# The first modulation's sums in chunks of two, modulation halves at other places, and attention units between the value blocks

## The chip, the cores and the metric

The kernel is one launch on one core of a Trainium2 chip. The metric is the device time of that launch in microseconds (us). TensorE is called PE below, VectorE DVE, ScalarE ACT, GpSimd POOL; SyncE (SP) issues nearly all of the transfers.

## The reference, cut to what matters

Two layers run over 384 tokens (128 of context, 256 latent) of 1024 channels. Each layer is a feed-forward block, a mixer with three head groups, and a second feed-forward block; nine modulation vectors per layer (from `c` for the latent tokens, from `c_ctx` for the context) scale and shift what goes in and gate what comes out.

```python
def _layer(x, cvec, lp, mixer):
    mod = jax.nn.silu(cvec) @ lp["ada_w"] + lp["ada_b"]
    sh1, sc1, g1, sh2, sc2, g2, sh3, sc3, g3 = jnp.split(mod[:, None, :], N_ADA, axis=-1)
    h = _rmsnorm(x, lp["norm_g"][0]) * (1.0 + sc1) + sh1
    x = x + 0.5 * g1 * _swiglu(h, lp["ffn_w1"][0], lp["ffn_w3"][0], lp["ffn_w2"][0])
    h = _rmsnorm(x, lp["norm_g"][1]) * (1.0 + sc2) + sh2
    y, ctx = mixer(h)
    x = x + g2 * y
    h = _rmsnorm(x, lp["norm_g"][2]) * (1.0 + sc3) + sh3
    x = x + 0.5 * g3 * _swiglu(h, lp["ffn_w1"][1], lp["ffn_w3"][1], lp["ffn_w2"][1])
    return x, ctx
```

The mixer projects `h` to a gated long convolution (Hyena, by Fourier transforms), a neighbourhood attention (kind "N", 6 heads, with a learned bias and a mask) and a windowed grouped-query attention (kind "G", 6 query heads), and projects their outputs back.

## The kernel before, in words

**Matmuls.** Every large fp32 matmul is three products of split operands (`mm3`, lines 305 to 307): high by high, low by high, high by low. A weight tile arrives in a `raw` buffer, ACT copies it to `whi` (L142), DVE subtracts to make `wlo` (L143). There are four `raw` buffers and the split runs three tiles ahead of its use; a `raw` buffer comes free when `wlo` is made. Activations are split the same way into `mh` and `ml`. Results stand in 8 PSUM buffers of two tags, "a" and "b", handed out in rotation: a buffer's next user waits until all readers of the last one are done. Each engine runs its instructions in the order in which the code writes them.

**Start of layer 0.** `start(j, mid)` runs at the head (and, with `mid`, in the middle) of step j of the first feed-forward block's first eight steps, in which six output blocks are summed over eight pieces of 128 channels. It has to make the normalised, modulated input `mh[j]` of each step. The first two modulation vectors are made on PE, in chunks of columns (`CHUNK`, 3, 3 and 2 blocks of 128 columns), and for each chunk twice, q = 0 for the scale and q = 1 for the shift: `chunk_load` issues the weights, `chunk_rows` (L278) multiplies them into rows, ACT copies the rows (L280), `chunk_cols` (L289) turns them into columns, and DVE makes `gsc` (L299, L300) or `mod` (L296). The squares of x are summed by ACT (L326) and DVE (L328); `stats1` sums them over partitions on PE (`pss`, L341) and makes the reciprocal roots on DVE (L313 to L320), `stats2` spreads these over the partitions (`dg` L347, `pr` L353, `R` L355). `start_x` (L1131) multiplies x by `R`, and `start_h` (L1122) applies `gsc` and `mod` on ACT and splits the result.

**The other modulation vectors.** They are made on DVE, a "half" at a time (L206, one row of 1024 products summed for one of the two vectors). `ada_tick(rate)` adds 2·rate halves of credit and issues the whole ones at that place; `need` issues what is still missing when a piece of the next stage asks for it. `RATE` holds the rates of the feed-forward blocks, `MIXRATE` those in the mixer, `SLOTADA` those in attention slots 6 and later.

**The mixer.** It projects block by block (`project`, each with a callback after each weight tile); background generators (`add`, `work`, `drain`) fill in filter, rotary and normalisation work. The last projection is that of the neighbourhood values, `vN`. After it come the attention units, 12 of them (three pairs of heads, two query halves, N first, then G), one started per `slot()`. Slot s issues the mask transfers of unit s+2, the scores of unit s on PE with DVE's row minima (L896), the normalisation of unit s-1 on DVE (`un_norm`, L870 and L873), the transposes of unit s-2 on PE with ACT's copies (L934, L939), the value products of a finished pair (L957, L960), and then the exponentials of unit s on ACT (L913 for the context part, L919). Units of the first query half (n = 2) have a context part, those of the second (n = 1) have none. The output projection follows in three groups of blocks (`wout_block`); `update` (L385) adds each block into x, and `after` does the squares, `need` and the input of the next block.

Of the kernel before, what the change touches and what calls it, by code (L numbers as in the profile page):

```python
# [27 lines left out]
NSPL = 4  # L28
AHEAD = 3
NADAB = 3  # L30
RATE = ((0.76, 0.635), (0.63, 0.515), (0.69, 0.66), (0.065, 0))
MIXRATE = ((0.75, 0, 0, 0), (0.45, 0, 0, 0))
BUD = (1.55, 3.3, 1.3)
SLOTADA = (6, 0.3, 0.0)
CHUNK = ((0, 3), (3, 6), (6, 8))
TAGS = (True, False, True)
GA = 2
DLATE = 8
# [21 lines left out]
for _name, _w in (  # L60
    ("ada_b", DEPTH * NADA * KD), ("norm_g", DEPTH * 3 * KD), ("conv_w", DEPTH * 3 * 6), ("conv_b", DEPTH * 6),
    ("skip", DEPTH * 2), ("naq", DEPTH), ("nak", DEPTH), ("fb1", DEPTH), ("fb2", DEPTH), ("freq", DEPTH * 2),
    ("fscale", 3), ("sel", 2),
):
    SM[_name] = (_n, _w)
    _n += _w
# [13 lines left out]
def _build(ctx, tc, nc, A):  # L80
# [181 lines left out]
    def chunk_load(c):  # L262
        a, b = CHUNK[c]
        n = (b - a) * P
        for q in range(2):
            firsts[c, q] = [tt("adw", w=NT) for _ in range(KD)]
            for k, t in enumerate(firsts[c, q]):
                load(A["ada0"][q, k, :, a * P:b * P], t[:, :n])

    adm = {}  # L270

    def chunk_rows(c, q):
        a, b = CHUNK[c]
        n = (b - a) * P
        pm = ps("adm", "ab"[q])
        for k, t in enumerate(firsts.pop((c, q))):
            o = 32 * (k % 4)
            T.matmul(pm[o:o + 32, :n], ct[:, k], t[:, :n], start=(k < 4), stop=(k >= 4))  # L278
        rows = tt("adr", w=NT)
        S.activation(rows[:, :n], pm[:, :n], AF.Copy)  # L280
        adm[c, q] = pm, rows

    def chunk_cols(c, q):
        a, b = CHUNK[c]
        n = b - a
        pm, rows = adm.pop((c, q))
        o = pm[:, NT:NT + 2 * n]
        for i in range(n):
            T.matmul(o[:, 2 * i:2 * i + 2], rows[:, i * P:(i + 1) * P], small("sel", 0, 2), start=True, stop=True)  # L289
        o = o.rearrange("p (j v) -> p j v", v=2)  # L290
# [4 lines left out]
        if q:
            V.tensor_tensor(mod[0][:, 0, a:b], o, wide(small("ada_b", a, n)), op=ALU.add)  # L296
        else:
            t = gsc[0][:, 0, a:b]
            V.tensor_tensor(t, o, wide(small("norm_g", a, n)), op=ALU.mult)  # L299
            V.tensor_tensor(t, t, wide(gb0[:, a:b]), op=ALU.add)  # L300
        done.update((0, 1 - q, j) for j in range(a, b))
# [234 lines left out]
    def mixer(l, after):  # L536
# [328 lines left out]
        def un_norm(u):  # L865
            nm, n = u.nm, u.n
            sums, rec = nm[:, 4:4 + 2 * n], nm[:, 12:12 + 2 * n]
            if u.kind == "G":
                V.tensor_tensor(sums, sums, nm[:, 8:8 + 2 * n], op=ALU.add)
            V.reciprocal(rec, sums)  # L870
            for e in range(2):
                for c, (pr, w) in enumerate(u.pr[e]):
                    V.tensor_scalar(pr[:, :w], pr[:, :w], rec[:, e * n + c:e * n + c + 1], None, op0=ALU.mult)  # L873

        def un_score(u):
            i, n = u.i, u.n
# [191 lines left out]
        drain(q_it)  # L1068
        drain(k_it)
        drain(conv_it)  # L1070
        drain(filt_it)
        fft_it = add(fft())
# [59 lines left out]

    def start(j, mid=False):
        if mid:
            if j in (2, 5):
                c = (j + 1) // 3
                chunk_cols(c, 1)
                for k in range(*CHUNK[c]):
                    start_h(k)
        elif j == 0:  # L1140
            chunk_load(0)
            issue(3)
# [11 lines left out]
            for c in range(3):  # L1154
                start_x(c, R)
                start_h(c)
            ahead(2)
            issue(4)
            chunk_load(2)
            for c in range(3, KD):  # L1160
                start_x(c, R)
        elif j in (1, 4):
            chunk_rows((j + 2) // 3, 0)
        elif j in (2, 5):
            chunk_cols((j + 1) // 3, 0)
            chunk_rows((j + 1) // 3, 1)
        elif j == 6:
# [95 lines left out]
def _layout(I):  # L1263
# [32 lines left out]
    put("sel", (np.arange(P)[:, None] % 32 == np.arange(2)[None]).astype(f32))  # L1296
    a["sml"] = sml
    rows = np.concatenate(
        [
# [75 lines left out]
```

## Time and profile before

| | us |
|---|---|
| median of 3 runs | 1543.95 (1543.29 to 1543.99) |
| profiled execution | 1544.34 |
| its span in the trace | 1542.6 |
| PE busy | 1505.7 (98%) |
| DVE busy | 1139.4 (74%) |
| ACT busy | 672.6 (44%) |
| POOL busy | 70.7 (5%) |

The span is what the trace covers; the profiled execution's own time is 1.74 us more. Terms below are set against 1544.34, which is 0.39 us above the median of the three runs. In a row of the timeline the first number is the start in us from the start of the span, the second the duration; "L305" is a line of the kernel, `xN` the number of instructions in the row, and the bracket at the end is how long the engine was idle before it and which instruction released it. PEclk is TensorE's granted clock as a share of full speed: 1.00 is 2.4 GHz, 0.50 is 1.2 GHz.

### The profile page before, as it was taken

What the parts mean: (1) busy time and instruction counts of PE and PEld (TensorE: products, weight loads), DVE (VectorE), ACT (ScalarE), POOL (GpSimd) and SP (SyncE); (2) the same over time, 40 slices, a digit from 0 to 9 for tenths busy, and PEclk for the clock granted to TensorE, in tenths of its full rate; (3) what the DMA queues carried; (4) which work ended last, traced back from release to release, by engine and by line L of the source; (5) the groups of instructions that cost most, each with busy time, mean ns of one, the idle gap of its engine ahead of it and who ended that gap; (6) DMA issues with size and microseconds to landing.
All of it is one profiled execution on the core that took longest, in us unless ns stands there. A gap on an engine that the chain in (4) does not pass through costs nothing. (4 is left out here: it accounts for less than half of the span.)

```text
span 1542.6 us, 23084 instructions
## 1 busy us (share of the span) xinstructions
PE 1505.7 (98%) x8652; PEld 1444.0 (94%) x8652; DVE 1139.4 (74%) x2158; ACT 672.6 (44%) x1234; POOL 70.7 (5%) x181
## 2 busy tenths in 40 slices
PE   6999999999989999999999999999999999999999
PEld 3999999999768999999999999999996699999998
DVE  4489888879787788877758898787897767544344
ACT  4533333446566454333434433343556655433221
POOL 0000000013300000000000000000141000000000
PEclk9999999999999999999999999999999999999999
DMA  9656665664403446555544565566543034343442
GB/s 307 236 184 237 219 223 201 218 195 149 129 30 117 153 148 220 207 212 187 187 162 139 188 244 209 207 221 202 172 124 109 26 111 138 134 149 108 149 152 72
DMA packets 89733, 261.27 MB, mean 169 GB/s; under 512 B 10097, under 2 KB 27796, under 8 KB 89492
## 3 DMA queue, kind: packets, MB, share of 16 engines
q1 hardware_dynamic: 89236, 258.74, 49.1%
q8 instruction: 68, 1.11, 0.3%
q0 software_dynamic: 384, 1.05, 0.2%
q14 instruction: 45, 0.37, 0.1%
HBM read 257.13 MB, written 2.62 MB: 168 GB/s over the span
## 5 line engine op out<-in xcount | busy, mean ns | idle before, releaser
L143 DVE TENSOR_TENSOR wlo<-raw,whi 128x1024 fp32r<-128x1024 f32 (+2 forms) x352 | 394.4, 1126 | 122.6 <-ACT whi L142 122.5
L305 PE MATMUL up<-mh,whi 128*128 128x384 f32 (+1 forms) x1408 | 479.3, 340 | 4.9 <-ACT mh L142 4.9
L306 PE MATMUL up<-ml,whi 128*128 128x384 f32 (+1 forms) x1408 | 477.4, 339 | 0.7 <-DVE ml L143 0.4
L307 PE MATMUL up<-mh,wlo 128*128 128x384 f32 (+1 forms) x1408 | 477.3, 339 | 0.8 <-DVE wlo L143 0.6
L142 ACT ACTIVATE whi<-raw 128x1024 fp32r<-128x1024 f32 (+2 forms) x352 | 338.4, 974 | 264.4 <-PE dn L306 128.2
L206 DVE CUSTOM_DVE_ANT_0 junk<-adaw,cb,sml 128x1024 bf16<-128x1024 f32 x256 | 332.7, 1300 | 1.9
L305 PEld LDWEIGHTS up<-mh,whi 128*128 128x128 f32 x1408 | 265.8, 189 | 8.7 <-ACT mh L142 6.3
L306 PEld LDWEIGHTS up<-ml,whi 128*128 128x128 f32 x1408 | 265.6, 189 | 2.5 <-DVE ml L143 2.1
L307 PEld LDWEIGHTS up<-mh,wlo 128*128 128x128 f32 x1408 | 266.0, 189 | 2.1 <-DVE wlo L143 2.1
L305 PE MATMUL dn<-gh,whi 128*128 128x384 f32 x704 | 237.4, 337 | 0.0
L306 PE MATMUL dn<-gl,whi 128*128 128x384 f32 x704 | 237.2, 337 | 0.0
L307 PE MATMUL dn<-gh,wlo 128*128 128x384 f32 x704 | 237.1, 337 | 0.0
L142 ACT ACTIVATE gh<-t 128x384 fp32r<-128x384 f32 x76 | 39.9, 525 | 273.0 <-DVE t L485 263.3
L307 PEld LDWEIGHTS dn<-gh,wlo 128*128 128x128 f32 x704 | 132.2, 188 | 0.0
L305 PEld LDWEIGHTS dn<-gh,whi 128*128 128x128 f32 x704 | 132.2, 188 | 0.0
L306 PEld LDWEIGHTS dn<-gl,whi 128*128 128x128 f32 x704 | 132.2, 188 | 0.0
L305 PE MATMUL pj<-whi,mh 128*128 128x384 f32 (+1 forms) x240 | 80.1, 334 | 1.0 <-DVE hyt L362 1.0
L485 DVE TENSOR_TENSOR t<-up,t 128x384 f32<-128x384 f32 x72 | 40.0, 556 | 55.0 <-PE up L307 54.8
L307 PE MATMUL pj<-whi,ml 128*128 128x384 f32 (+1 forms) x240 | 78.3, 326 | 0.0
L306 PE MATMUL pj<-wlo,mh 128*128 128x384 f32 (+1 forms) x240 | 78.2, 326 | 0.0
L143 DVE TENSOR_TENSOR gl<-t,gh 128x384 fp32r<-128x384 f32 x76 | 42.5, 559 | 45.0 <-ACT gh L142 45.0
L326 ACT ACTIVATE sq<-xT 128x384 f32<-128x384 f32 x42 | 22.0, 525 | 100.6 <-DVE xT L385 99.3
(222 smaller groups left out, 1582.9 us busy)
## 6 DMA issues: line engine op xcount, KB each, us to landing
raw<-w SPq DMA_DIRECT2D x184, 512.0 KB, 4.4
adaw<-ada SPq DMA_DIRECT2D x128, 512.0 KB, 3.5
raw<-w SPq DMA_DIRECT2D x64, 448.0 KB, 4.3
raw<-win SPq DMA_DIRECT2D x48, 384.0 KB, 4.0
raw<-w13a SPq DMA_DIRECT2D x32, 384.0 KB, 4.0
adw<-ada SPq DMA_DIRECT2D x32, 192.0 KB, 4.3
raw<-woa SPq DMA_DIRECT2D x16, 384.0 KB, 3.2
nab<-nab SPq DMA_DIRECT2D x24, 192.0 KB, 2.5
```

The costliest lines, as they stand in the source:

```text
L142: S.activation(hi, src, AF.Copy)
L143: V.tensor_tensor(lo, src, hi.bitcast(F32), op=ALU.subtract)
L206: V.tensor_tensor_reduce(out=junk, in0=w, in1=cb[:, v, :], scale=scale, scalar=small("ada_b", (l * NADA + p) * KD + j), op0=ALU.mult, op1= ...
L305: T.matmul(out, ah, bh, start=start, stop=False)
L306: T.matmul(out, ah, bl, start=False, stop=False)
L307: T.matmul(out, al, bh, start=False, stop=stop)
L326: S.activation(sq, xT[j], AF.Square)
L485: V.tensor_tensor(t1, PQ[1][:, :NT], t1, op=ALU.mult)
```

## The change

Three places change. Line numbers of the changed kernel are 2 lower than before in the helpers (303 to 305 are the three products, 278 and 289 stay).

**The start.** There are four chunks of two column blocks. Both vectors of a chunk go through one PSUM buffer, so that one `chunk_rows` (16 matmuls of 256 columns) and one `chunk_cols` (2 matmuls) make both. The sum of squares and the statistics on DVE stand ahead of the first chunk's rows. In the loop the rows of chunk 1, 2, 3 stand in the middle of steps 1, 3, 5 and the columns, with `start_h`, at the head of steps 2, 4, 6.

```diff
-CHUNK = ((0, 3), (3, 6), (6, 8))
+CHUNK = ((0, 2), (2, 4), (4, 6), (6, 8))
...
+            r = stats1(V)
+            chunk_rows(0)
+            R = stats2(r)
             ada_tables(0)
-            chunk_rows(0, 0)
-            r = stats1(V)
-            chunk_cols(0, 0)
-            chunk_rows(0, 1)
-            R = stats2(r)
-            chunk_cols(0, 1)
+            start_x(0, R)
+            chunk_cols(0)
             ahead(1)
...
+        if j in (2, 4, 6):
+            chunk_cols(j // 2)
+            start_h(j)
+            start_h(j + 1)
```

PE's order from the start of the program to the first product of step 0, before (`adm` is the modulation's PSUM buffer, `adw` the weights, `adr` the rows, `up` an output block of the feed-forward block):

```order
L278 MATMUL adm<-adw,cb 32x384 x8
L341 MATMUL pss<-ones,accq 128x1 x3
L289 MATMUL adm<-sml,adr 128x2 x3
L278 MATMUL adm<-adw,cb 32x384 x8
L353 MATMUL pr<-dg,ones 128x384
L289 MATMUL adm<-sml,adr 128x2 x3
L305 MATMUL up_369<-mh_112,whi 128x384
```

and now:

```order
L339 MATMUL pss<-ones,accq 128x1 x3
L278 MATMUL adm<-adw,cb 32x256 x16
L351 MATMUL pr<-dg,ones 128x384
L289 MATMUL adm<-sml,adr 128x4 x2
L303 MATMUL up_358<-mh_112,whi 128x384
```

The sum of squares moved from between the two sets of rows to the head, and one set of columns is left between `pr` and the first product.

PE's order around the columns of the second chunk before: they stand in the middle of step 2, between products of the same `mh_114`.

```order
L306 MATMUL up_371<-ml_122,whi 128x384
L307 MATMUL up_371<-mh_114,wlo 128x384
L289 MATMUL adm<-sml,adr 128x2 x3
L305 MATMUL up_372<-mh_114,whi 128x384
L306 MATMUL up_372<-ml_122,whi 128x384
```

Now they stand directly ahead of the first product that uses `mh_114`, which is made from them:

```order
L304 MATMUL up_363<-ml_121,whi 128x384
L305 MATMUL up_363<-mh_113,wlo 128x384
L289 MATMUL adm<-sml,adr 128x4 x2
L303 MATMUL up_358<-mh_114,whi 128x384
L304 MATMUL up_358<-ml_122,whi 128x384
```

**The modulation halves of layer 0.** The rates of its first feed-forward block go up, the ticks in the slots go, and the blocks of the output projection's second and third group get a rate of 0.3.

```diff
-RATE = ((0.76, 0.635), (0.63, 0.515), (0.69, 0.66), (0.065, 0))
-MIXRATE = ((0.75, 0, 0, 0), (0.45, 0, 0, 0))
+RATE = ((0.82, 0.72), (0.63, 0.515), (0.69, 0.66), (0.065, 0))
+MIXRATE = ((0.75, 0, 0, 0.3), (0.45, 0, 0, 0))
-SLOTADA = (6, 0.3, 0.0)
...
-            if s >= SLOTADA[0]:
-                ada_tick(SLOTADA[1 + l])
```

DVE's order in layer 0's output projection before, ahead of the fourth block of x (`xT_87`; `wlo` are the low parts of the next weight tiles, `accq` the sum of squares):

```order
L143 TENSOR_TENSOR wlo<-raw,whi 128x768
L143 TENSOR_TENSOR wlo<-raw,whi 128x1024 x2
L143 TENSOR_TENSOR wlo<-raw,whi 128x768
L385 SCALAR_TENSOR_TENSOR xT_87<-po_4940,mod_106,xT_87 128x128
L385 SCALAR_TENSOR_TENSOR xT_87<-po_4940,mod_106,xT_87 128x256
L328 TENSOR_TENSOR accq<-accq,sq 128x384
```

and now (a half is the two rows of L205, with `junk` and `mod` as its outputs):

```order
L142 TENSOR_TENSOR wlo<-raw,whi 128x768
L205 ISA junk,mod_106<-adaw,cb,sml 128x1024
L205 ISA mod_106 128x1
L142 TENSOR_TENSOR wlo<-raw,whi 128x1024
L205 ISA junk,mod_106<-adaw,cb,sml 128x1024
L205 ISA mod_106 128x1
L142 TENSOR_TENSOR wlo<-raw,whi 128x1024
L142 TENSOR_TENSOR wlo<-raw,whi 128x768
L205 ISA junk,mod_106<-adaw,cb,sml 128x1024
L205 ISA mod_106 128x1
L383 SCALAR_TENSOR_TENSOR xT_87<-po_4982,mod_106,xT_87 128x128
```

Three halves now stand between these low parts and the fourth block. At the seventh block (`xT_90`) DVE had before:

```order
L143 TENSOR_TENSOR wlo<-raw,whi 128x768 x2
L385 SCALAR_TENSOR_TENSOR xT_90<-po_5075,mod_106,xT_90 128x128
L385 SCALAR_TENSOR_TENSOR xT_90<-po_5075,mod_106,xT_90 128x256
L206 ISA junk,gsc_108<-adaw,cb,sml 128x1024
L206 ISA gsc_108 128x1
L225 TENSOR_TENSOR gsc_108<-gsc_108,sml 128x2
L206 ISA junk,mod_106<-adaw,cb,sml 128x1024
L206 ISA mod_106 128x1
L206 ISA junk,mod_106<-adaw,cb,sml 128x1024
L206 ISA mod_106 128x1
L328 TENSOR_TENSOR accq<-accq,sq 128x384
```

and now:

```order
L142 TENSOR_TENSOR wlo<-raw,whi 128x768 x2
L205 ISA junk,mod_106<-adaw,cb,sml 128x1024
L205 ISA mod_106 128x1
L383 SCALAR_TENSOR_TENSOR xT_90<-po_5124,mod_106,xT_90 128x128
L383 SCALAR_TENSOR_TENSOR xT_90<-po_5124,mod_106,xT_90 128x256
L326 TENSOR_TENSOR accq<-accq,sq 128x384
```

Five halves behind the seventh and the eighth block went; four now stand further ahead, three between the `wlo` of the second group and the fourth block, one ahead of the seventh.

**Attention, in both layers.** Slots 0 and 1 run after the second and the third weight tile of `vN`, behind the rest of the query and key work; and for units of the second query half the normalisation of the second head goes to ACT.

```diff
+                    if n == 1 and e:
+                        S.activation(pr[:, :w], pr[:, :w], AF.Copy, scale=r)
+                    else:
...
-        vN = project(384, 2, whole)
+        def first_units(kb):
+            whole(kb)
+            if kb == 1:
+                drain(q_it)
+                drain(k_it)
+            if kb in (1, 2):
+                slot()
+
+        vN = project(384, 2, first_units)
```

PE's order at the first scores of layer 0 before (`pj` a value block, `kf` and `gk` background work, `sc` scores):

```order
L307 MATMUL pj_4004<-whi,ml_127 128x384
L621 MATMUL kf<-ts,dft_2950 128x256
L621 MATMUL kf<-ts,dft_2951 128x256
L621 MATMUL kf<-td,dft_2952 128x256
L621 MATMUL kf<-td,dft_2953 128x256
L885 MATMUL sc_4201<-kTN_3424,qTN_3695 128x384
L885 MATMUL sc_4202<-kTN_3424,qTN_3695 128x384
L888 MATMUL sc_4201<-kTN_3430,qTN_3695 128x128
L888 MATMUL sc_4202<-kTN_3430,qTN_3695 128x128
L885 MATMUL sc_4229<-kTN_3424,qTN_3695 128x384
```

and now:

```order
L887 MATMUL sc_4166<-kTN_3476,qTN_3747 128x384
L887 MATMUL sc_4167<-kTN_3476,qTN_3747 128x384
L890 MATMUL sc_4166<-kTN_3482,qTN_3747 128x128
L890 MATMUL sc_4167<-kTN_3482,qTN_3747 128x128
L751 MATMUL gk<-ident,pj 128x128
L751 MATMUL gk<-ident,ra 128x128 x2
L619 MATMUL kf<-ts,dft_3000 128x256
L619 MATMUL kf<-ts,dft_3001 128x256
L619 MATMUL kf<-td,dft_3002 128x256
L619 MATMUL kf<-td,dft_3003 128x256
L619 MATMUL kf<-ts,dft_3002 1x256
L619 MATMUL kf<-ts,dft_3003 1x256
```

The first scores moved from behind the last value block to ahead of its third tile, and the background matmuls that take PSUM buffers of the same tag stand behind them. On ACT the table load and the first exponentials now stand between background copies:

```order
L620 ACTIVATE K_3364<-kf,sml 1x256
L915 ACT_TABLE_LOAD
L915 ACTIVATE pr_4173,nm<-sc_4166,nm 128x128
L915 ACTIVATE pr_4173,nm<-sc_4167,nm 128x128
L921 ACTIVATE pr_4174,nm<-pr_4174,nm 128x384
L921 ACTIVATE pr_4175,nm<-pr_4175,nm 128x384
L1058 ACTIVATE kTG_3670<-gk 128x128
L1059 ACTIVATE kTG<-gk 128x256
```

where before they stood behind the last background copies of the value blocks:

```order
L724 ACTIVATE pj<-pj_4004 128x384
L622 ACTIVATE K_3308<-kf,sml 128x256
L622 ACTIVATE K_3311<-kf,sml 128x256
L913 ACT_TABLE_LOAD
L913 ACTIVATE pr_4208,nm<-sc_4201,nm 128x128
L913 ACTIVATE pr_4208,nm<-sc_4202,nm 128x128
```

What stands behind the exponentials on ACT (the copies of `kTG` and `K`) thus moved behind a wait for the first scores' row minima, which need the first mask.

## Rows read from the trace of the kernel before

**Rows 1.** The page's busy time of each engine over the span.

```profile
PE 1505.7 (98%) x8652; PEld 1444.0 (94%) x8652; DVE 1139.4 (74%) x2158; ACT 672.6 (44%) x1234; POOL 70.7 (5%) x181
```

**Rows 2.** Busy time by stretch: from and to (us), length, then for PE, PE's weight loads, DVE, ACT and POOL the busy us and the instructions, then PEclk, the share of the DMA engines that was busy, GB/s.

```profile
26.00:30.00 4.00, 4.00 (x14) 4.00 (x14) 1.42 (x3) 2.45 (x5) 0.00 (x0) 0.50 1.03 344
...
424.00:430.00 6.00, 4.93 (x20) 3.24 (x18) 5.89 (x22) 4.18 (x14) 0.00 (x0) 0.55 0.53 168
430.00:480.00 50.00, 45.77 (x312) 33.84 (x309) 43.06 (x140) 30.11 (x88) 0.00 (x0) 1.00 0.11 38
...
518.00:522.00 4.00, 3.86 (x14) 3.83 (x14) 2.54 (x6) 1.43 (x2) 2.09 (x7) 0.57 0.97 373
```

**Rows 3.** The timeline of the start, up to the first product of step 0.

```profile
9.10 1.22 DVE L328 TENSOR_TENSOR accq<-accq,sq 128x384 f32<-128x384 f32 x2
20.13 0.91 PE L353 MATMUL pr<-dg,ones 128*128 128x384 f32 x2 [0.34 <-DVE dg L347]
21.08 0.49 ACT L355 ACTIVATE R<-pr 128x384 f32<-128x384 f32 x1 [0.76 <-PE pr L353]
23.79 0.98 ACT L1122 ACTIVATE xr<-xr,mod,gsc 128x128 f32<-128x128 f32 x2 [1.50 <-DVE xr L1131]
25.38 0.69 PE L305 MATMUL up<-mh,whi 128*128 128x384 f32 x1 [3.78 <-ACT mh L142]
```

**Rows 4.** SP's transfers at the start (start, time over which they were issued, count).

```profile
5.93 9.01 SPq L104 DMA_DIRECT2D adw<-ada  x16
```

**Rows 5.** The same timeline at the last columns before, around 53 us, with one set of rows.

```profile
50.43 1.07 PE L278 MATMUL adm<-adw,cb 128*32 128x256 f32 x16
53.12 0.50 PE L289 MATMUL adm<-sml,adr 128*128 128x2 f32 x4
53.73 0.16 DVE L296 TENSOR_TENSOR mod<-adm,sml 128x4 f32<-128x4 f32 x1 [2.84 <-PE adm L289]
55.53 0.44 PE L305 MATMUL up<-mh,whi 128*128 128x384 f32 x1 [0.23 <-ACT mh L142]
```

**Rows 6.** Matmuls of the modulation between 26 and 56 us, by shape: busy us, mean ns.

```profile
L278 PE MATMUL adm<-adw,cb 128*32 128x384 f32 x32 | 3.0, 492 | 0.0
L289 PE MATMUL adm<-sml,adr 128*128 128x2 f32 x20 | 2.5, 234 | 0.0
L278 PE MATMUL adm<-adw,cb 128*32 128x256 f32 x32 | 2.1, 385 | 0.0
```

**Rows 7.** DVE's busy time by stretch in the first feed-forward block of layer 0 (columns as in rows 2).

```profile
100.00:160.00 60.00, 60.00 (x345) 60.00 (x344) 53.67 (x81) 22.36 (x31) 0.00 (x0) 1.00 0.62 219
...
220.00:314.00 94.00, 94.00 (x540) 94.00 (x539) 75.36 (x128) 35.82 (x60) 0.00 (x0) 1.00 0.62 214
```

**Rows 8.** The same places of the attention in layer 0 and layer 1: the PE rows with a wait before them.

```profile
421.53 0.55 PE L934 MATMUL pp<-ident,pr 128*128 128x128 f32 x3 [1.47 <-DVE pr L873]
425.52 1.51 PE L934 MATMUL pp<-ident,pr 128*128 128x128 f32 x6 [1.07 <-DVE pr L873]
...
475.15 0.44 PE L957 MATMUL py<-PT,vG 128*64 128x128 f32 x4 [0.20 <-DVE yl L143]
...
1176.43 0.55 PE L934 MATMUL pp<-ident,pr 128*128 128x128 f32 x3 [1.47 <-DVE pr L873]
1180.43 1.51 PE L934 MATMUL pp<-ident,pr 128*128 128x128 f32 x6 [0.65 <-ACT pr L913]
...
1228.72 0.44 PE L957 MATMUL py<-PT,vG 128*64 128x128 f32 x4 [0.38 <-DVE yl L143]
```

**Rows 9.** DVE's timeline in layer 0's output projection, PE's wait behind it, and the same sum in layer 1.

```profile
482.07 0.74 DVE L385 SCALAR_TENSOR_TENSOR xT<-po,mod,xT 128x128 f32<-128x128 f32 x2
491.72 4.18 DVE L143 TENSOR_TENSOR wlo<-raw,whi 128x768 fp32r<-128x768 f32 x4 [0.20 <-ACT whi L142]
505.48 1.83 DVE L143 TENSOR_TENSOR wlo<-raw,whi 128x768 fp32r<-128x768 f32 x2 [0.20 <-ACT whi L142]
507.88 1.33 DVE L206 CUSTOM_DVE_ANT_0 junk<-adaw,cb,sml 128x1024 bf16<-128x1024 f32 x1
516.07 0.55 DVE L328 TENSOR_TENSOR accq<-accq,sq 128x384 f32<-128x384 f32 x1
516.77 0.80 PE L341 MATMUL pss<-ones,accq 128*128 128x1 f32 x6 [2.65 <-DVE accq L328]
...
1235.45 0.74 DVE L385 SCALAR_TENSOR_TENSOR xT<-po,mod,xT 128x128 f32<-128x128 f32 x2
1265.05 0.56 DVE L328 TENSOR_TENSOR accq<-accq,sq 128x384 f32<-128x384 f32 x1 [0.59 <-ACT sq L326]
```

**Rows 10.** The first unit in layer 0: masks on SP, the first row minimum on DVE, table load and exponentials on ACT.

```profile
407.66 19.74 SPq L104 DMA_DIRECT2D nab<-nab  x12
...
416.42 1.28 ACT L913 ACT_TABLE_LOAD   x1
416.93 0.56 DVE L896 CUSTOM_DVE_ANT_0 pr<-sc,nab 128x384 f32<-128x384 f32 x1 [2.71 <-PE sc L888]
417.74 0.37 ACT L913 ACTIVATE pr<-sc,nm 128x128 f32<-128x128 f32 x1
```

**Rows 11.** A summary of the mask transfers in layer 0 (400 to 420 us): time from issue to landing, least, median, most.

```profile
DMA to landing us min/median/max: 2.3/4.4/4.7
```

**Rows 12.** DVE's normalisations between 415 and 480 us: busy us, mean ns.

```profile
L873 DVE TENSOR_SCALAR pr<-pr,nm 128x384 f32<-128x384 f32 x24 | 9.5, 418 | 0.4
```

More of the change, by code (lines that the diff above doesn't have):

```diff
@@ L62 @@
     ("skip", DEPTH * 2), ("naq", DEPTH), ("nak", DEPTH), ("fb1", DEPTH), ("fb2", DEPTH), ("freq", DEPTH * 2),
-    ("fscale", 3), ("sel", 2),
+    ("fscale", 3), ("sel", 4),
 ):
@@ L264, in chunk_load, with chunk_rows @@
         n = (b - a) * P
[L265 to L268, printed above, removed]
+        firsts[c] = [[tt("adw", w=NT) for _ in range(2)] for _ in range(KD)]
+        for k in range(KD):
+            for q in range(2):
+                load(A["ada0"][q, k, :, a * P:b * P], firsts[c][k][q][:, :n])
     adm = {}
-    def chunk_rows(c, q):
+    def chunk_rows(c):
@@ L273, in chunk_rows @@
         a, b = CHUNK[c]
         n = (b - a) * P
[L275 to L278, printed above, removed]
+        pm = ps("adm", "a")
+        for k, w in enumerate(firsts.pop(c)):
+            for q in range(2):
+                o = 64 * q + 32 * (k % 2)
+                T.matmul(pm[o:o + 32, :n], ct[:, k], w[q][:, :n], start=(k < 2), stop=(k >= KD - 2))
@@ L279, in chunk_rows, with chunk_cols @@
         rows = tt("adr", w=NT)
         S.activation(rows[:, :n], pm[:, :n], AF.Copy)
-        adm[c, q] = pm, rows
-    def chunk_cols(c, q):
+        adm[c] = pm, rows
+    def chunk_cols(c):
         a, b = CHUNK[c]
         n = b - a
-        pm, rows = adm.pop((c, q))
-        o = pm[:, NT:NT + 2 * n]
+        pm, rows = adm.pop(c)
+        o = pm[:, NT:NT + 4 * n]
         for i in range(n):
-            T.matmul(o[:, 2 * i:2 * i + 2], rows[:, i * P:(i + 1) * P], small("sel", 0, 2), start=True, stop=True)
-        o = o.rearrange("p (j v) -> p j v", v=2)
+            T.matmul(o[:, 4 * i:4 * i + 4], rows[:, i * P:(i + 1) * P], small("sel", 0, 4), start=True, stop=True)
+        o = o.rearrange("p (j q v) -> p j q v", q=2, v=2)
@@ L292, in wide @@
         def wide(t):
             return t.rearrange("p (j o) -> p j o", o=1).to_broadcast([P, n, 2])
[L295 to L301, printed above, removed]
+        t = gsc[0][:, 0, a:b]
+        V.tensor_tensor(t, o[:, :, 0], wide(small("norm_g", a, n)), op=ALU.mult)
@@ L303, in mm3 @@
+        V.tensor_tensor(t, t, wide(gb0[:, a:b]), op=ALU.add)
+        V.tensor_tensor(mod[0][:, 0, a:b], o[:, :, 1], wide(small("ada_b", a, n)), op=ALU.add)
+        done.update((0, p, j) for p in range(2) for j in range(a, b))
     def mm3(out, a, b, start, stop):
@@ L872, in un_norm @@
                 for c, (pr, w) in enumerate(u.pr[e]):
-                    V.tensor_scalar(pr[:, :w], pr[:, :w], rec[:, e * n + c:e * n + c + 1], None, op0=ALU.mult)
+                    r = rec[:, e * n + c:e * n + c + 1]
+                    if n == 1 and e:
+                        S.activation(pr[:, :w], pr[:, :w], AF.Copy, scale=r)
+                    else:
+                        V.tensor_scalar(pr[:, :w], pr[:, :w], r, None, op0=ALU.mult)
         def un_score(u):
@@ L1065, in mixer @@
         gq_it = add(gq_post(pg))
-        vN = project(384, 2, whole)
+        def first_units(kb):
[6 more added lines that the diff above has]
+        vN = project(384, 2, first_units)
         nc.gpsimd.dma_start(out=A["o_nv"][l], in_=vN[0])
-        drain(q_it)
-        drain(k_it)
         drain(conv_it)
@@ L1134, in start @@
         if mid:
[L1135 to L1140, printed above, removed]
+            if j in (1, 3, 5):
+                chunk_rows((j + 1) // 2)
+            return
+        if j == 0:
             chunk_load(0)
-            issue(3)
+            issue(2)
             chunk_load(1)
@@ L1145, in start @@
                 square_chunk(c)
+            r = stats1(V)
+            chunk_rows(0)
+            R = stats2(r)
             ada_tables(0)
-            chunk_rows(0, 0)
-            r = stats1(V)
-            chunk_cols(0, 0)
-            chunk_rows(0, 1)
-            R = stats2(r)
-            chunk_cols(0, 1)
+            start_x(0, R)
+            chunk_cols(0)
             ahead(1)
-            for c in range(3):
-                start_x(c, R)
-                start_h(c)
+            start_h(0)
+            start_x(1, R)
+            start_h(1)
             ahead(2)
@@ L1159, in start @@
             chunk_load(2)
-            for c in range(3, KD):
+            for c in range(2, KD):
                 start_x(c, R)
[L1162 to L1167, printed above, removed]
+            return
+        if j in (2, 4, 6):
+            chunk_cols(j // 2)
+            start_h(j)
+            start_h(j + 1)
+        if j == 2:
+            chunk_load(3)
+        if j == 6:
             load(A["fw1"], fw1)
@@ L1295, in _layout @@
     put("fscale", fscale)
-    put("sel", (np.arange(P)[:, None] % 32 == np.arange(2)[None]).astype(f32))
+    row, col = np.arange(P)[:, None], np.arange(4)[None]
+    put("sel", ((row // 64 == col // 2) & (row % 32 == col % 2)).astype(f32))
     a["sml"] = sml
```

## The prediction

> **What bounds the kernel.** I read the busy times first: PE works for 98% of the span, DVE for 74%, ACT for 44% [rows 1]. So time is saved only where PE waits, where PE runs work that another order needs less of, or where its clock is low. Of PE's waits that the change touches there are four groups: the wait of 3.78 us ahead of the first product, at 21.6 us [rows 3]; the small ones while the first block's chunks are made [rows 5]; the attention's, for normalised rows [rows 8]; and 2.65 us for the sum of squares in layer 0 [rows 9]. Behind the long ones the clock is at 1.2 GHz for a while: PEclk 0.50 from 26 to 30 us, 0.55 from 424 to 430, 0.57 from 518 to 522 [rows 2]. All of this together is some tens of us in 1543, and the change moves parts of it, not the bulk.
>
> **The start, up to the first product.** Before, the first chunk is 16 transfers whose issue spans 9.01 us [rows 4], and the second set of rows, `pr` and the columns wait for the last of them; `pr` stands at 20.13 and the first product at 25.38 [rows 3]. The chunk now has two thirds of the bytes, so at the same rate its last transfer is 9.01 / 3 = 3.0 us earlier; and the squares, done at 10.32 (9.10 + 1.22) [rows 3], no longer wait behind rows on PE, so that the statistics overlap the transfers. I put `pr` 3.8 us earlier, at 16.3. From `pr` to the first product it is 5.25 us before; a low part of a weight tile (0.96 us on DVE, from 1.83 for two [rows 9]) no longer stands ahead of the first `xr`, so 4.25. First product at 20.55, 4.8 us earlier; bounds 3.0 (the transfers alone) and 5.5.
> It then runs at the low clock for a time. Before that was from 25.38 until 30.0 [rows 2, 3]; behind the wait at 514 it was about 3.4 us of matmuls. Taking 3.4, some 1.2 us less at half speed is a gain of 0.5; bounds 0 and 1.
>
> **The start, steps 0 to 5.** Before, rows cost 3.0 + 2.1 = 5.1 us and columns 2.5 [rows 6], waits about 0.6: 8.2 in all. The columns stood in the middle of a step, so that what follows them was hidden behind nine products, of which only 0.23 us showed at step 6 [rows 5]. Now rows are three sets of 16 at 1.07 = 3.2, columns three times at most 0.5 = 1.5. But the columns of each chunk stand directly ahead of the product that needs them, and nothing else is in PE's queue. From the end of the columns (53.62) to the first product that hangs on them (55.53) it was 1.91 us [rows 5]: DVE 0.16, ACT twice, with hand-overs. Now DVE does three operations there, not one, 0.19 each with their hand-over: 1.91 + 0.38, and 0.15 for the columns' shorter overlap: 2.44. Three of these are 7.3. New sum 3.2 + 1.5 + 7.3 = 12.0, so 3.8 is lost.
> A wait of 2.44 with only columns ahead of it is near the one of 2.65 with only the sum's matmuls behind it [rows 9], after which the clock was down: (1 - 0.57) x 4.00 = 1.7 us lost [rows 2]. Three waits thus cost between 0 and 5.1; the chunk's waits are shorter and I take one of the three, 1.7.
> The start in all: 4.8 + 0.5 - 3.8 - 1.7 = -0.2, a loss of 0.2, with bounds of -4.6 and +2.7.
>
> The Trainium skill ("TensorE: Matmul & The Clock Gate", section "Why this matters for your kernels") asks for no long idle gaps of PE between bursts of matmuls, with a limit that 2.44 us would keep within. By it none of the three waits would cost clock. The row at 516.77 speaks against it: 2.65 us of wait, which the limit also allows, had 0.57 behind it.
>
> **The halves of layer 0.** The five in slots 6 and later go. What they cost is read from the two layers, since layer 1 has none there: from the transposes at 421.53 and 1176.43 (754.90 apart) to the products at 475.15 and 1228.72 (753.57 apart) layer 0 takes 1.3 us more [rows 8]. Gain 1.3; bounds 0.5 and 1.5.
> The five behind the seventh and eighth blocks also go, and that looks like the end of the 2.65 us wait and its low clock, 2.65 + 1.7 = 4.35. I don't count it. DVE and ACT are a chain there, block by block, and in it the four low parts at 491.72 stand back to back, 4.18 us with 0.20 before them [rows 9]. Three halves put between them add 3 x 1.33 = 4.0, the fourth ahead of the seventh block another 1.3: 5.3. Layer 1 shows the chain without halves: 1235.45 to 1265.61, 30.2 us; with 5.3 it is 35.5, against 34.5 before (482.07 to 516.62) [rows 9]. The sum comes 1.0 late. And the two low parts at 505.48 come 4.0 late; the first of them was done at 506.4 and step 1 of the second block wants it at about 507.8 (the wait began at 514.12; three steps of 18 products of 0.176 us ahead of it began at 504.6). PE thus waits 2.6 there, and at the sum 0.9 more instead of 2.65. Loss 0.8, bounds -1.5 and +4.35.
> The rest of the halves goes into the first block by its higher rates. DVE is at 53.67 of 60 us in its first part and 75.36 of 94 in its second, while PE is full [rows 7]. A rate 8% higher in the first part adds at most 4.3 us to 53.67, one 13% higher adds at most 10 to 75.36: both stay below the stretch, with tiles split three ahead. Nothing, and if the cover were gone, the 4.3 less the 6.3 that are free, so still nothing.
>
> **Attention, both layers.** What goes: 1.47 + 1.07 in layer 0, 1.47 + 0.65 in layer 1 [rows 8], and the low clock behind them: 4.93 us of PE's work at 0.55 [rows 2] can give 2.2 at most, nothing if DVE sets the pace; I take 1.0, as DVE is at 43.06 of 50 us afterwards. What comes: PE now meets matmuls of the background with PSUM buffers that the first scores held (first scores, then `kf`, as the order shows). These wait for the first exponentials, ACT for DVE's minima, and DVE for the mask. Masks are issued on SP behind the raw tiles, at 407.66 before [rows 10]; one weight tile earlier that is about 404.8, and it lands 2.3 to 4.7 us after its issue [rows 11]: about 408. From the first minimum's start to the end of the first context exponential it was 1.18 us (416.93 to 417.74 + 0.37) [rows 10]; with the second of each I take twice that, 2.4, so 410.4. The scores themselves would be done about 1 us before the mask lands (an estimate, from the place of the first masks' issue between the same tiles), so PE stands for 3.4 us, bounds 1 and 5. With a low clock behind it in one case of two, 0.9. The table load, 1.28 us [rows 10], is on ACT ahead of the exponentials and lies beside the wait for the mask.
> Six normalisations of 0.418 [rows 12] leave DVE for ACT in each layer, 2.5 us; since DVE sets much of the pace, I take 1.5, bounds -2 (ACT's copies for PE then stand behind the normalisation, and PE waits for ACT) and 2.5.
> Layer 0: 2.54 + 1.0 - 3.4 - 0.9 + 1.5 = 0.7. Layer 1: 2.12 + 1.0 - 3.4 - 0.9 + 1.5 = 0.3. Together a gain of 1.0, bounds -8 and +8.
>
> The Trainium skill ("ScalarE: Activation LUTs", section "What ACT_TABLE_LOAD costs") adds a drain of about 1.4 us to the load itself. By it the slot's wait could be 1.4 us longer in each layer. The trace disagrees: the exponential starts at 417.74, right behind the load's end at 417.70.
>
> **Sum.** -0.2 + 1.3 - 0.8 + 1.0 = 1.3 us less. The profiled execution took 1544.34, so 1543.0, 0.9 below the median of the runs. A change of less than 0.2%, 3.1 us, can't be told from none here.
>
> **Rivals.**
> *The tail hides its halves.* If the halves fall into DVE's pauses between the blocks, the wait at 514 and its low clock go: 1543.0 - 4.35 - 0.8 = 1537.9. For it: layer 1 has no wait at that place [rows 9]. Against: three of the four stand where DVE has no pause. Chance 0.13.
> *The mask is there in time.* Then the stall at the first slot is about 1 us and leaves the clock alone: 2.4 + 0.9 less per layer, 6.6 in both: 1536.4. For it: transfers that landed in 2.3 us [rows 11]. Against: before, the issue waited for free raw tiles, and still does. Chance 0.20.
> *The clock stays up in the start.* If none of the three waits in steps 2, 4 and 6 brings the clock down, the 1.7 comes back: 1541.3. For it: the waits are a little shorter than the one of 2.65 us; against it, that this one did. Chance 0.15. This is what the Trainium skill's rule on gaps (named above) would make of it.
> *Slower: the value blocks stall twice.* The minima stand in DVE's queue ahead of the low parts of the next value tiles, so a late mask holds back these as well, and slot 1 repeats the stall: 3.4 more per layer and 0.8 of clock, 8.4 in both: 1551.4. It decides the sign once the waits between the value tiles exceed about 6 us per layer. For it: one queue, no other work between. Against: the second mask is issued right behind the first. Chance 0.17.
> The forecast as it stands has 0.35.
>
> **Chances and range.** Faster by over 0.2% (below 1540.9): 0.13 + 0.20, and 0.05 each from the forecast and the clock's case: 0.43. Slower (above 1547.0): 0.17 and 0.03 of the forecast: 0.20. Within: 0.37. The likeliest one's own range is 1540 to 1547. The range takes in both faster cases with 1.4 for the start's bounds, to 1535, and half of the slower one's way, to 1549.
>
> **What would show it.** First product near 20.5; three waits of 2 to 3 us at steps 2, 4, 6, ending with ACT's `mh`, and PEclk behind each; PE's wait between the second and the third value tile, released by ACT's exponentials; no halves from 440 to 480; DVE's halves at the `wlo` of the output projection, and PE waiting for a low part at step 1 of layer 0's second block. The forecast is wrong if the first product is later than 22.5, if the value blocks run without a stall, or if the second block's first three steps run through.

## The result and the profile after

The changed kernel takes 1565.62 us (median of 4, 1564.07 to 1566.72), against 1543.75 for the kernel before in the same comparison: a ratio of 1.0141 (95% interval 1.0124 to 1.0159), 21.9 us slower. The forecast was 1543.0, with a range of 1535 to 1549: it named a small gain and was 22.6 us off.

The page's busy times, which answer to [rows 1]:

```profile
PE 1509.5 (97%) x8668; PEld 1448.2 (93%) x8668; DVE 1136.1 (73%) x2149; ACT 672.3 (43%) x1244; POOL 69.0 (4%) x181
```

The span grew by 19.7 us (1542.6 to 1562.3) and PE's busy time by 3.8: the other 15.9 us are PE standing. PE's waits show where. First the start (timeline of PE, rows with a wait, and the row of `pr`), against [rows 3, 5]:

```profile
17.88 0.91 PE L351 MATMUL pr<-dg,ones 128*128 128x384 f32 x2
21.88 0.44 PE L303 MATMUL up<-mh,whi 128*128 128x384 f32 x1 [2.75 <-ACT mh L141]
...
36.27 0.47 PE L303 MATMUL up<-mh,whi 128*128 128x384 f32 x1 [3.03 <-ACT mh L141]
49.16 0.44 PE L303 MATMUL up<-mh,whi 128*128 128x384 f32 x1 [2.10 <-ACT mh L141]
...
62.68 0.44 PE L303 MATMUL up<-mh,whi 128*128 128x384 f32 x1 [2.60 <-ACT mh L141]
```

The first product is 3.5 us earlier (21.88 for 25.38), and step 6, which began at 55.53, begins at 62.68: the six steps lost 10.6 us. The three long waits stand at steps 2, 4 and 6, each released by ACT's `mh`. Behind each of them the clock is down, as the stretches of the same kernel show (columns as in [rows 2]):

```profile
36.00:40.00 4.00, 3.60 (x11) 3.32 (x12) 1.12 (x2) 1.62 (x4) 0.00 (x0) 0.57 0.88 280
...
50.00:54.00 4.00, 4.00 (x15) 4.00 (x15) 1.52 (x2) 1.26 (x2) 0.00 (x0) 0.57 0.93 345
...
64.00:68.00 4.00, 4.00 (x16) 4.00 (x15) 1.78 (x2) 2.97 (x5) 0.00 (x0) 0.59 0.97 363
```

PEclk of 0.57, 0.57 and 0.59 over 4 us each leave 0.43, 0.43 and 0.41 of each stretch unused: 5.1 us of full speed lost, an estimate that takes PE as the bound there. By line, PE's modulation work from 20 to 64 us is this (busy us, mean ns), against [rows 6]:

```profile
L278 PE MATMUL adm<-adw,cb 128*32 128x256 f32 x96 | 5.8, 382 | 0.0
L289 PE MATMUL adm<-sml,adr 128*128 128x4 f32 x12 | 1.6, 240 | 0.2 <-ACT adr L280 0.2
```

It is 7.4 us where it was 7.6 in the steps. But it is for six blocks of columns now and was for five, since the first chunk makes two blocks ahead of the first product and not three. So a block costs less than before, and the steps as a whole got no lighter.

Then the attention. PE's rows with a wait in layer 1, to be read against the last three of [rows 8] and against this row of the kernel before, which has the only wait for ACT's copies in this stretch:

```profile
1214.86 0.97 PE L885 MATMUL sc<-kTG,qTG 64*128 64x384 f32 x3 [0.84 <-ACT PT L939]
```

and after:

```profile
1192.63 0.85 PE L936 MATMUL pp<-ident,pr 128*128 128x128 f32 x6 [1.62 <-DVE pr L875]
1196.02 0.44 PE L789 MATMUL pz<-ident,uc 128*128 128x128 f32 x2 [1.82 <-ACT PT L941]
...
1225.35 0.49 PE L819 MATMUL cv<-dft,ya 128*128 128x128 f32 x2 [1.45 <-ACT PT L941]
1230.34 0.49 PE L819 MATMUL cv<-dft,ya 128*128 128x128 f32 x2 [0.84 <-ACT PT L941]
1239.15 1.40 PE L887 MATMUL sc<-kTG,qTG 64*128 64x384 f32 x4 [2.49 <-ACT PT L941]
```

Four of the waits, 6.6 us in place of 0.84, end with ACT's copies of the transposes (`PT`), which free PE's PSUM buffers. ACT's timeline around the first of them tells why the copies are late:

```profile
1192.12 0.61 ACT L873 ACTIVATE pr<-pr,nm 128x384 f32<-128x384 f32 x1 [3.52 <-DVE nm L868]
1192.64 1.06 ACT L941 ACTIVATE PT<-pp 128x512 f32<-128x512 f32 x2
```

The normalisation moved to ACT (L873) waits 3.52 us for DVE's reciprocal (L868), and the copies stand in the queue behind it. The summary of that line counts 33.2 us of ACT's waiting for the reciprocal over its 12 instructions, 2.8 us each:

```profile
L873 ACT ACTIVATE pr<-pr,nm x12: 614/615/617, 432.1 to 1246.1; 128x384 f32<-128x384 f32 x12
...
  DVE nm L868: 33.2, 12
```

The wait at the first slot, which the forecast put at 3.4 us and at a late mask, is 1.34 in both layers, and the mask is there: DVE's first minimum waits for the scores. What PE waits for is the first exponential, and ahead of it on ACT stands the table load, which itself began only behind DVE's minimum (0.87 us of idle, released by DVE), as the rows of DVE, ACT and PE show:

```profile
414.12 0.56 DVE L898 CUSTOM_DVE_ANT_0 pr<-sc,nab 128x384 f32<-128x384 f32 x1 [0.58 <-PE sc L890]
414.96 1.28 ACT L915 ACT_TABLE_LOAD   x1 [0.87 <-DVE nm L903]
416.77 1.13 PE L619 MATMUL kf<-td,dft 128*128 128x256 f32 x4 [1.34 <-ACT pr L915]
```

### The profile page after: what moved, and what is told of

The parts are those of the page before. It is cut to its first block, busy times and chain, and to the rows that moved or that the text cites. A ratio compares the mean times of both kernels' runs of the same rounds, so it can differ in the third digit from the quotient of the medians.

```text
span 1562.3 us, 23143 instructions
## 1 busy us (share of the span) xinstructions
PE 1509.5 (97%) x8668; PEld 1448.2 (93%) x8668; DVE 1136.1 (73%) x2149; ACT 672.3 (43%) x1244; POOL 69.0 (4%) x181
## 4 chain that ended last, share of the span: by engine, by line
PE 83%; DVE 7%; ACT 6%; issue 2%; DMA 1%; SPq 1%; POOL 0%; DVEq 0%; ACTq 0%; POOLq 0%
PE up L304 15%; PE up L305 15%; PE up L303 15%; PE dn L304 8%; PE dn L305 8%; PE dn L303 8%; PE pj L303 3%; PE pj L305 2%; PE pj L304 2%; DVE wlo L142 1%; ACT whi L141 1%; DVE pr L898 1%; DVE ml L142 1%; PE hy L303 1%; PE hy L304 1%
## 5 line engine op out<-in xcount | busy, mean ns | idle before, releaser
L205 DVE CUSTOM_DVE_ANT_0 junk<-adaw,cb,sml 128x1024 bf16<-128x1024 f32 x256 | 332.6, 1299 | 2.0
L303 PEld LDWEIGHTS up<-mh,whi 128*128 128x128 f32 x1408 | 266.8, 189 | 15.6 <-ACT mh L141 12.1
L324 ACT ACTIVATE sq<-xT 128x384 f32<-128x384 f32 x42 | 21.9, 525 | 114.3 <-DVE xT L383 113.0
```

The source lines that it names most:

```text
L205: V.tensor_tensor_reduce(out=junk, in0=w, in1=cb[:, v, :], scale=scale, scalar=small("ada_b", (l * NADA + p) * KD + j), op0=ALU.mult, op1= ...
L303: T.matmul(out, ah, bh, start=start, stop=False)
```

## The experiments

First each of the four parts alone on the kernel before, all on one chip, where the kernel before took 1544.57. The edits are the parts of the diff shown above.

**The new start alone.** 

> The kernel before with the new start alone. Theory (the chunk's waits at steps 2, 4, 6 cost more than the earlier first product gives): first product 3.5 us earlier, but about 7.7 us of waits and three falls of the clock at 1.6 to 1.7 us each; 8 to 9 us slower, about 1552.5. Rival (the start is about even, and the time is lost in the mixers alone): 1543 to 1545.

Measured: 1553.62, ratio 1.0058 (1.0043 to 1.0073), 9.0 us slower. The waits are those of the changed kernel: 2.82, 2.10 and 2.58 us ahead of steps 2, 4, 6. The theory holds.

**The halves alone.** 

> The kernel before with the modulation halves of layer 0 at the new places alone. Theory (the halves put between the low parts of the output projection cost there what they saved behind it): within 1 us of before or up to 2 us faster by the slots, 1542 to 1544.5. Rival (they are hidden in the output projection): the wait of 2.65 us and the low clock behind it go, and the slots give 1.3: about 1538.

Measured: 1543.55, ratio 0.9996 (0.9987 to 1.0006): no difference. The tail of layer 0 in PE's timeline, against the single wait of 2.65 in [rows 9]:

```profile
506.64 0.44 PE L304 MATMUL up<-mh,whi 128*128 128x386 f32 x1 [1.23 <-ACT whi L141]
507.63 0.44 PE L306 MATMUL up<-mh,wlo 128*128 128x386 f32 x1 [0.38 <-DVE wlo L142]
514.73 0.80 PE L340 MATMUL pss<-ones,accq 128*128 128x1 f32 x6 [0.80 <-DVE accq L327]
516.12 0.45 PE L304 MATMUL up<-mh,whi 128*128 128x386 f32 x1 [0.59 <-ACT whi L141]
517.11 0.69 PE L306 MATMUL up<-mh,wlo 128*128 128x386 f32 x1 [0.33 <-DVE wlo L142]
```

One wait of 2.65 became five, 3.3 us together: the weight splits come later than before, as the forecast had it. The clock falls there as it did: PEclk is 0.82 from 514 to 518 us and 0.75 from 518 to 522, which is 1.7 us of full speed, what the 0.57 of [rows 2] cost. The 1.3 us that the halves in the slots should give are not told apart from none.

**The normalisation alone.**

```diff
+                    if n == 1 and e:
+                        S.activation(pr[:, :w], pr[:, :w], AF.Copy, scale=r)
+                    else:
```

> The kernel before with the normalisation of the second head of the second query halves on ACT alone. Theory (ACT's normalisation waits for DVE's reciprocal behind the next unit's minima, and the copies for PE wait behind it): PE waits of 1 to 2.5 us at the copies in three or four slots of each layer, 4 to 6 us per layer, about 1552 to 1556. Rival (DVE sets the pace there, and is relieved; the loss is from the early slots): 0 to 3 us faster, 1541 to 1544.

Measured: 1562.76, ratio 1.0122 (1.0107 to 1.0138), 18.2 us slower. Worse than the theory had it, and by far the largest part. The two attention stretches, first of the kernel before and then of this run:

```profile
415.00:485.00 70.00, 63.23 (x397) 46.32 (x396) 58.09 (x188) 44.40 (x128) 0.00 (x0) 0.95 0.21 68
1170.00:1240.00 70.00, 64.37 (x406) 48.10 (x405) 53.15 (x181) 44.85 (x130) 0.00 (x0) 0.95 0.17 53
...
415.00:485.00 70.00, 58.02 (x330) 40.15 (x329) 50.03 (x170) 41.17 (x124) 0.00 (x0) 0.88 0.13 39
1170.00:1240.00 70.00, 58.77 (x346) 42.17 (x346) 47.85 (x164) 42.29 (x124) 5.07 (x15) 0.95 0.21 62
```

PE loses 5.2 and 5.6 us of busy time in them, and in layer 0 also a share of its clock. PE's rows name two kinds of wait, for the copies (`PT`) and for the exponentials (`pr`, L917); both stand behind the moved normalisation in ACT's queue:

```profile
435.43 0.33 PE L753 MATMUL gt<-ident,pj 128*128 128x128 f32 x1 [2.03 <-ACT pr L917]
475.25 1.40 PE L889 MATMUL sc<-kTG,qTG 64*128 64x384 f32 x4 [2.29 <-ACT PT L943]
...
1201.08 0.47 PE L753 MATMUL gt<-ident,pj 128*128 128x128 f32 x1 [3.03 <-ACT pr L917]
1237.17 1.40 PE L889 MATMUL sc<-kTG,qTG 64*128 64x384 f32 x4 [1.09 <-ACT PT L943]
```

Over both layers' attention the waits for copies grew from 1.7 to 7.3 us and those for exponentials from 0.7 to 7.0. So the theory names one half of the wait; the exponentials are the other.

**The early slots alone.** 

> The kernel before with the first two slots between the value tiles alone. Theory (the first slot's wait for the mask costs about what the two waits before the first transposes cost): 0 to 2 us faster per layer, 1540 to 1544. Rival (the early slots block the value tiles, and the loss of some 6 us per layer is theirs): about 1555.

Measured: 1541.06, ratio 0.9979 (0.9969 to 0.9988), 3.5 us faster. The page's busy times (to be read against [rows 1]) and the stretches that hold the attention:

```profile
PE 1499.7 (97%) x8652; PEld 1439.5 (94%) x8652; DVE 1138.9 (74%) x2158; ACT 670.9 (44%) x1234; POOL 69.5 (5%) x181
...
405.00:475.00 70.00, 62.45 (x401) 45.16 (x399) 57.72 (x188) 44.93 (x131) 4.11 (x14) 1.00 0.18 59
1158.00:1228.00 70.00, 63.58 (x412) 46.54 (x409) 53.33 (x181) 45.97 (x133) 4.30 (x15) 1.00 0.19 60
```

PE works 6.0 us less for the same 8652 matmuls and stands 2.2 us longer (the span is 1538.8). So no waiting was saved: the waits of [rows 8] were replaced by others (1.34, 1.63 and 0.47 us at the start of layer 0's attention). What changed is the speed of the matmuls, and PEclk is 1.00 where it was 0.95 in the same stretches of the kernel before. Yet the clock may not be all of it. Three executions of the kernel before had a granted clock of 0.997 or 0.998 over the whole span, and took 1542.83, 1543.23 and 1543.63; the six of this run at 0.996 or 0.997 took 1539.64 to 1541.23. Some 2 us are left between executions of like clock, and where they come from stays open.

The four parts add up to 9.0 - 1.0 + 18.2 - 3.5 = 22.7 us; the whole change measured 21.9.

**Is it the place in ACT's queue?** The next run, and three with other bases, shared a kernel before of 1544.73. ACT's copies of unit s-2 are issued ahead of the normalisation of unit s-1:

```diff
-            if 0 <= s - 1 < len(hs):
-                un_norm(hs[s - 1])
             if 0 <= s - 2 < len(hs):
                 un_turn(hs[s - 2])
+            if 0 <= s - 1 < len(hs):
+                un_norm(hs[s - 1])
```

> As the run with the normalisation alone on ACT, but ACT's copies for the transposes of unit s-2 are issued ahead of the normalisation of unit s-1. Theory (the time is lost because the copies stand behind a normalisation that waits for DVE): the waits for these copies go, 1544 to 1550. Rival (ACT has too much to do, or the exponentials behind the normalisation are what PE waits for): 1555 or more, with the waits at other instructions.

Measured: 1548.26, ratio 1.0022 (1.0013 to 1.0032). With the same work on the same engines, the order alone gives back some 14.7 of the 18.2 us. (On the kernel before the same swap would change nothing: the normalisation there is DVE's alone, the transposes and copies are PE's and ACT's.) ACT's waiting for the reciprocal falls from 34.6 to 15.6 us. The 3.5 left say that ACT's share is still no gain: PE's rows of layer 1 still show waits for exponentials (0.98 and 0.48 us, where the run with the normalisation alone had 3.03 at the first of the two places).

```profile
1189.97 0.33 PE L753 MATMUL gt<-ident,pj 128*128 128x128 f32 x1 [0.98 <-ACT pr L917]
...
1223.15 0.90 PE L938 MATMUL pp<-ident,pr 128*128 128x128 f32 x6 [0.48 <-ACT pr L917]
```

**The start with its columns covered.** Rows at the head of steps 1, 3, 5, columns in their middle:

```diff
         if mid:
             if j in (1, 3, 5):
-                chunk_rows((j + 1) // 2)
+                chunk_cols((j + 1) // 2)
+                start_h(j + 1)
+                start_h(j + 2)
             return
...
-        if j in (2, 4, 6):
-            chunk_cols(j // 2)
-            start_h(j)
-            start_h(j + 1)
+        if j in (1, 3, 5):
+            chunk_rows((j + 1) // 2)
```

> The kernel before with the new start, but rows of a chunk at the head of steps 1, 3, 5 and columns with the inputs made from them in the middle of the same steps, behind which nine products stand. Theory (the loss is the three exposed waits with their clock falls): the waits of 2.1 to 2.8 us and the three falls go, some 10 us faster than the new start alone, 1540 to 1543, if the second chunk has landed by step 1; else up to 2 us of wait there. Rival (the start is bound by the transfers of chunks and weights, whatever the place of the columns): 1550 or more, with PE waiting for transfers.

Measured: 1545.07, ratio 1.0004 (0.9995 to 1.0013): 8.6 us faster than the new start alone, and no faster than before.

```profile
22.78 0.44 PE L304 MATMUL up<-mh,whi 128*128 128x384 f32 x1 [2.75 <-ACT mh L142]
...
33.00 0.61 PE L290 MATMUL adm<-sml,adr 128*128 128x4 f32 x4 [1.20 <-ACT adr L281]
35.77 0.44 PE L304 MATMUL up<-mh,whi 128*128 128x384 f32 x1 [0.49 <-ACT mh L142]
45.72 0.44 PE L304 MATMUL up<-mh,whi 128*128 128x384 f32 x1 [0.48 <-ACT mh L142]
...
51.92 0.62 PE L279 MATMUL adm<-adw,cb 128*32 128x256 f32 x2 [0.53 <-DMA adw<-ada]
56.80 0.45 PE L304 MATMUL up<-mh,whi 128*128 128x384 f32 x1 [0.50 <-ACT mh L142]
```

The long waits were the loss. But the first product's lead of 2.6 us is gone again by step 6 (56.80 for 55.53): the inputs come 0.5 us late at steps 2, 4 and 6, where the kernel before had 0.22 and 0.23 at its two places, and twice the next chunk's weights or rows were late (0.53 and 1.20 us of wait).

**The two good parts together, and with that start.** 

> The kernel before with the early slots and the new places of the halves together, without the new start and without the normalisation on ACT. Theory (the parts are independent): -3.5 and -1.0 against before, about 1540. Rival (they share DVE's spare time): 1541 to 1543.

Measured: 1538.76, ratio 0.9963 (0.9949 to 0.9977), 6.0 us faster than before. The parts' sum is 4.5; by the intervals the two can't be told apart.

> The same with the new start that has its columns in the middle of steps. Theory: the sum of the parts, about 1536 to 1539. Rival (transfers bind the start): slower than the run without the start.

Measured: 1540.29, ratio 0.9973 (0.9963 to 0.9984): 1.5 us behind the run without it. On both bases the covered start gains nothing.

**The normalisation at the end of its slot.** On the early slots and the halves (kernel before on this chip: 1544.45), ACT's part is issued behind the exponentials:

```diff
             if s < len(hs):
                 un_exp(hs[s])
+            while after_exp:
+                pr, r = after_exp.pop()
+                S.activation(pr, pr, AF.Copy, scale=r)
```

> The early slots and the new places of the halves, with the normalisation on ACT put behind the copies and behind the exponentials of its slot. Theory (only its place in ACT's queue was at fault; DVE is relieved of 2.5 us per layer): no waits for copies beyond those of the run without it, 1537 to 1540, the same as that run or up to 2 us faster. Rival (ACT has no room for 0.6 us more in these slots): 2 to 5 us slower than that run, 1541 to 1544.

Measured: 1550.73, ratio 1.0038 (1.0024 to 1.0052), 12 us behind the same kernel with the normalisation on DVE. The theory, that only the place ahead of the copies was at fault, falls. PE's rows of layer 1 name the wait: the next transposes need the normalised row itself (L997). In the two profiled executions PE stands 4.6 us longer than without ACT's part, and works 7.0 us longer for the same 8652 matmuls.

```profile
1184.42 0.55 PE L939 MATMUL pp<-ident,pr 128*128 128x128 f32 x3 [1.06 <-ACT pr L997]
...
1225.56 0.55 PE L939 MATMUL pp<-ident,pr 128*128 128x128 f32 x3 [1.10 <-ACT pr L997]
1234.45 0.55 PE L939 MATMUL pp<-ident,pr 128*128 128x128 f32 x3 [0.62 <-ACT pr L997]
```

**The statistics first, with chunks of three.** On the same base:

```diff
+            r = stats1(V)
             ada_tables(0)
             chunk_rows(0, 0)
-            r = stats1(V)
+            R = stats2(r)
+            start_x(0, R)
             chunk_cols(0, 0)
             chunk_rows(0, 1)
-            R = stats2(r)
             chunk_cols(0, 1)
...
```

> The early slots and the new places of the halves, with the chunks of three as before, but the sum of squares ahead of the first chunk's rows, the spreading of the roots between its two sets of rows, and the first input's product ahead of the first low part on DVE. Theory (of the new start the order of the statistics is a gain of 1 to 2 us, and its chunks of two are the loss): first product 1 to 2 us earlier, 1537 to 1538. Rival (the last columns set the first product, and all of the gain was the smaller chunk): the same as the run without it, 1538.8, within 0.5.

Measured: 1538.68, ratio 0.9964 (0.9951 to 0.9977). Its first product is at 23.66, 1.7 us earlier than in [rows 3], yet the median is that of the run without it, on another chip. In the profiled executions the lead is still there: step 6 begins at 53.57, against 56.15 in the run without it, and the spans are 1535.6 and 1537.7. But these two lie at the fast end of five executions and near the slow end of five, so the medians decide, and by them the 1.7 us are not shown to reach the end.

**Two checks.** On a chip with the kernel before at 1544.61: the normalisation between copies and exponentials on the better base, and the changed kernel with only the normalisation taken back.

> The early slots and the new places of the halves, with the normalisation on ACT behind the copies and ahead of the exponentials. Theory (ACT's place is what counts: between copies and exponentials it costs 3 to 4 us, as it did on the kernel before, and behind the exponentials it holds back the next slot's transposes): 1541 to 1544. Rival (with the early slots ACT has no room at any place): 1549 or more, like the run with it behind the exponentials.

Measured: 1545.74, ratio 1.0006 (0.9997 to 1.0016). It lies between theory and rival: 5 us better than behind the exponentials, 7 worse than on DVE. None of the three places in ACT's queue that were tried gives a gain.

> The changed kernel with the normalisation back on DVE: new start, new places of the halves, early slots. Theory (the normalisation on ACT is 18 of the 22 us lost; the parts add up): 1544.5 + 9.0 - 1.0 - 3.5 = 1549, or 9.0 above the 1538.8 without the new start, 1547.8. Rival (the parts hang together, and the loss of the normalisation is smaller beside the early slots): 1553 or more.

Measured: 1547.12, ratio 1.0014 (1.0004 to 1.0024). That is 2.5 us slower than its own kernel before, where the whole change was 21.9 slower: taking back one part of the change gives back 19.4 of it. The theory's lower sum, 1547.8, is near.

## Why the prediction was wrong

- **The normalisation** was the step that failed. The forecast took 1.5 us of gain per layer from DVE's relief, with a bound of -2 for "ACT's copies for PE then stand behind the normalisation, and PE waits for ACT". That mechanism is the one that happened, with the exponentials held back beside the copies, but it costs 9 per layer, 18.2 in all for a forecast gain of 3.0. The gain was worked out from the instruction's own duration on DVE (six of 0.418), and the bound of -2 from no row at all. What ACT's queue stands behind is a wait for DVE, 2.8 us on average. The order already showed it: the reciprocal comes behind the next unit's minima on DVE, and ACT's copies, which free PSUM, behind the normalisation. I priced a moved instruction by its own duration, not by its wait.
- **The start's waits** were right in place and nearly in size: 2.44 forecast, 3.03, 2.10 and 2.60 measured, 7.7 for 7.3. The clock fell behind all three, not one: 5.1 for 1.7. The 0.5 for a shorter low clock at the beginning is not settled: PEclk from 20 to 36 us is 0.79 before, 0.89 in the changed kernel and again 0.79 in the new start alone. The first product came 3.5 earlier, not 4.8 (`pr` at 17.88, not 16.3). And the rows' work was mis-sized: I took 1.07 us for 16 matmuls from [rows 5], but its "x16" counts two matmuls of the trace for each of the program's, so a set of 16 in the program's order takes 1.93. Three sets are 5.8, not 3.2. In all -9.0 for the forecast's -0.2, outside its bound of -4.6. That bound is itself not the sum of its terms: 3.0 + 0 - 3.8 - 5.1 is -5.9.
- **The halves** were right in kind: no gain in the tail, for the reason given. At step 1 PE waits 1.23 and 0.38 us for a weight tile's parts where 2.6 was forecast, and 0.80 at the sum for 0.9. The parts 1.3 and -0.8 sum to 0.5; measured 1.0, with an interval that holds zero.
- **The early slots** were forecast at a loss without the normalisation (2.54 + 1.0 - 3.4 - 0.9 is -0.8 in layer 0, and -1.2 in layer 1). They gain 3.5 for both. The stall is 1.34, not 3.4: the mask was there, and the table load, which I had put beside the wait for it, came behind DVE's minimum. The clock did not fall behind the stall, for which I had charged 0.9 per layer. The 2.54 and 2.12 of waits that were to go did not come as a gain: other waits took their place. The bounds of -8 and +8 for the attention have no working, and the measured parts, -18.2 and +3.5, come to -14.7, outside them.
- **The rivals.** The slower one had the sign, but neither the size (1551.4) nor the place: value blocks that stall twice. They don't; the value tiles run on behind 1.34 us. *The mask is there in time* was right for its part: a stall of about 1 us and no fall of the clock, 6.6 better than the forecast of the early slots; they came out 5.4 better (3.5 for -1.9). *The clock stays up* and *the tail hides its halves* did not happen.
- **The signs of being wrong** did not fire: the first product came ahead of 22.5, the value blocks had a stall, and PE waited for weight tiles in the second block's first steps. No sign watched ACT's queue, where the largest loss was.

## What to carry to other kernels

An instruction moved to another engine's queue can cost that queue its whole wait, and hold back all that stands behind it: ask what it waits for, and who needs the next instructions, before counting what the first engine saves. Where PE bounds the kernel and an order makes it wait, give a fall of its clock a chance and a price as well: here the clock fell behind the waits of 3.03, 2.10 and 2.60 us in the start and behind one of two of 2.5 in the attention. Before a duration is multiplied, check that the trace's count and the program's count are of the same thing.

## What the runs showed of the hardware

The clock fell behind waits of 2.10 and 2.60 us at steps 4 and 6, shorter than the 2.65 of [rows 9]. But the length of a wait is not enough to tell. In the changed kernel PE waits 2.50 us at 476.6 in layer 0 and 2.49 at the same place of layer 1, and PE's, DVE's and ACT's busy times are nearly alike; the clock falls behind the first and not behind the second:

```profile
476.00:480.00 4.00, 1.50 (x9) 0.73 (x6) 2.23 (x12) 2.02 (x5) 0.00 (x0) 1.00 0.00 0
480.00:484.00 4.00, 4.00 (x17) 3.43 (x15) 3.29 (x13) 4.00 (x17) 0.00 (x0) 0.57 0.00 0
...
1236.00:1240.00 4.00, 1.51 (x11) 0.73 (x6) 2.22 (x12) 2.00 (x5) 0.00 (x0) 1.00 0.00 0
1240.00:1244.00 4.00, 4.00 (x26) 3.53 (x24) 3.31 (x13) 4.00 (x17) 0.00 (x0) 1.00 0.01 4
```

These rows don't say what differs; from them a term for it can only be a chance. And the moved normalisation takes 0.615 us on ACT for the 0.418 that it took on DVE [rows 12].
